# Two-layer hybrid encoder, one core: in layer 2 the weight sums of the seven-product pairs are built in a DRAM scratch by adding DMAs

## The chip, the cores and the metric

The kernel runs on one core of a Trainium2 chip. The metric is the device time of one execution in microseconds (us); the time before is the median of three runs, 1300.78 us (1300.57 to 1301.51). The engines are PE (TensorE, matrix products), DVE (VectorE), ACT (ScalarE), POOL (GpSimd) and SP (SyncE, which here only issues DMAs). Each works through its own queue of instructions in order.

## The reference, cut to what matters

Two encoder layers over 512 positions of width 1024, all in fp32. The change touches only how the third block of layer 2 gets its weights:

```python
for l in range(DEPTH):                      # DEPTH = 2
    x = x + hybrid_mixer(rms_norm(x, ...))              # neighbourhood attention || GQA, then W_out
    x = x + memory_cross_attention(rms_norm(x, ...))    # 4 heads over 256 memory tokens
    x = x + conv_ffn(rms_norm(x, ...), w_up[l], ..., w_down[l])
return rms_norm(x, norm_final)

def conv_ffn(h, w_up, conv_w, conv_b, w_down):          # D_FF = 2816 = 22 chunks of 128
    u = h @ w_up                                        # (512, 1024) @ (1024, 5632)
    u = depthwise_conv_width_3(u)
    gate, val = split(u, 2)
    return (silu(gate) * val) @ w_down
```

## The kernel before

**Arithmetic.** Activations lie transposed, features on the 128 partitions and the 512 positions along the row. PE multiplies in a reduced format (fp32r), so each operand is split into two: `hi` is a rounded copy (ACT), `lo` is the rest, value minus `hi` (DVE or POOL), and a product is three matmuls, hi·hi, hi·lo and lo·hi. Every weight block goes this way: SP loads it from DRAM into a `raw` tile (three buffers, N_RAW), ACT writes `hi`, DVE or POOL subtracts to `lo`, PE uses both. Tiles named `hi` and `lo` have four buffers each (N_W); tiles named `r` and `t` come from wider pools. `plan` lists all weight blocks in the order of use, with a letter for how each is split; `get_w` takes the next block and emits the loads and splits of the blocks ahead.

**The up-projection.** Of the 22 chunks j, the first six of each layer (N_PLAIN) are done as they stand: 48 matmuls of 512 columns for `gate` and `val` together. The other 16 are done as pairs, by a seven-product scheme: `gate` and `val` of a chunk, the two halves of the 1024 input features, and the two halves of the positions make a 2×2 times 2×2 product of blocks, done with seven block products instead of eight, each 4 × 3 matmuls of 256 columns (`product`). The scheme needs seven left operands made of weights: three blocks as they are (`11`, `12`, `22`) and four sums (`s1` to `s4`), and right operands `t1` to `t4` made of activations at the start of the stage (`operands`). In `up(j)` the products run in the order 11, s1, (22 of the pair before), s2, 12, s4, s3. By output tile and left operand they show in the trace as `tr<-r`, `sc<-r,hi`, `tr<-r`, `tr<-r,lo`, `sc<-r`, `sc<-r,hi`, `tr<-r,lo`.

**The weights of a pair.** A pair takes two loads of 512 KB, `first` (letter A) and `second` (letter B). `combined` then splits the three blocks with ACT and DVE (`r<-raw`), lets POOL make the four sums (two adds `t<-raw,raw`, two adds `t<-t,raw`), and splits those with ACT and DVE into halves of `hi` and `lo` tiles (`hi<-t`, `lo<-t`; the DVE half reads what ACT wrote, so it shows as `hi<-t,hi` and `lo<-t,lo`). Beside each pair comes one block of the down-projection (`down_grouped`, 24 matmuls of 512 columns, letter D).

**What sets the order.** All calls are recorded on a `Tape`. `Tape.plan` then runs a list scheduler over the whole program with assumed costs per instruction (`Step`) and with due times counted back from PE's work, in several variants, and `Tape.play` issues the instructions of each engine in the order of the best. So one edit may reorder every queue, also far from where it is made. During attention a `Filler` puts pieces of the projections between the attention steps, so that PE has work while ACT, DVE and POOL do the softmax.

Of the kernel before, what the change touches and what calls it, by code (L numbers as in the profile page):

```python
# [30 lines left out]
D_FF = 2816  # L31
NF = D_FF // P
N_GROUPED = 16
N_PLAIN = 6
N_RAWS = 3
N_COLS = 256
BEHIND = 5
# [64 lines left out]
class Step:  # L102
# [5 lines left out]
    def __init__(self, i, engine, name, call, args, kwargs):  # L108
        self.i, self.engine, self.name, self.call = i, engine, name, (call, args, kwargs)
        self.reads, self.writes = [], []  # L110
        for n, a in [*enumerate(args), *kwargs.items()]:
            if hasattr(a, "tensor") or type(a).__name__ == "Tile":
                a = a if hasattr(a, "ap") and not callable(a.ap) else a[:]
                (self.writes if n in (0, "out", "accum_out") else self.reads).append(a)
        self.needs, self.frees, self.after, self.leads = set(), set(), set(), set()
        self.opens, self.tiles, self.moved = [], [], 0
        if name == "dma_start":
            self.busy = self.length = 450.0
            to, source = self.writes[0], self.reads[0] if self.reads else None
            runs = min(run(a) for a in (to, source) if a is not None)  # L120
            inside = source is not None and type(source.tensor).__name__ == type(to.tensor).__name__ == "Tile"
            rate = 205.0 if to.shape[0] < P or inside else 285.0 if runs < 256 else 340.0 if runs < 512 else 375.0
            self.moved = 4 / rate
            for c in to.shape:
                self.moved *= c
        elif name == "make_identity":
            self.busy = self.length = 1200.0
        else:
            self.busy, self.length = self.times()
        ends = self.reads[:: max(1, len(self.reads) - 1)] if name in TWO_INPUTS else self.reads[:1] + self.writes  # L130
        self.shared = engine == E_POOL and columns(self.writes[0]) > 8 or (
            engine == E_DVE and (name in TWO_INPUTS or name in FAST and (name == "tensor_copy" or columns(self.writes[0]) > 4))
            and all(tag_of(a.tensor) not in IN_PSUM for a in ends))
# [48 lines left out]
class Tape:  # L182


    def __init__(self):
        self.steps, self.tag, self.users, self.opened = [], {}, {}, {}
        self.written, self.read, self.in_order = {}, {}, None

    def take(self, engine, name, call, args, kwargs):
        s = Step(len(self.steps), engine, name, call, args, kwargs)  # L190
        for a, w in [(a, False) for a in s.reads] + [(a, True) for a in s.writes]:
            if type(a.tensor).__name__ == "Tile":
                self.touch(s, a, w)
        if self.in_order is not None and s.moved:
            s.after.update(self.in_order[-1:])
            self.in_order.append(s.i)
        s.needs.discard(s.i)
        s.after -= s.needs | {s.i}
        for x in s.needs:
            self.steps[x].frees.add(s.i)  # L200
        for x in s.after:
# [298 lines left out]
def encoder_kernel(ctx: ExitStack, tc: tile.TileContext, t: dict, out: list):  # L500
# [66 lines left out]
    def operand_of(v, tile, sub):  # L567

# [66 lines left out]
    def stored(*shape):  # L635
        nonlocal at
        n = P * int(np.prod(shape))
        at += n
        v = t["w"][at - n : at]
        return v.rearrange("(p k c) -> p k c", p=P, c=shape[1]) if shape[1:] else v.rearrange("(p c) -> p c", p=P)  # L640

    firsts = [stored(n[2], P) if isinstance(n, tuple) else stored(S + 1) if isinstance(n, int) else
              stored(S // 2 + (n.stop == S)) for n in FIRST]
    for key, name, l, rows, c0, ncol, eng in weights():
        plan.append((key, stored(rows.shape[1], ncol) if len(plan) > 2 else None, rows.shape[1], ncol, eng))

    def get_wide(name):
        return [get_w((name, kq), min(AHEAD, 3 - kq)) for kq in range(4)]
# [263 lines left out]
    for l in range(DEPTH):  # L912
# [608 lines left out]
        def up_first():  # L1521


            us = [[None] * 2 for _ in range(N_PLAIN)]
# [18 lines left out]
            for j in range(2, N_PLAIN):  # L1543
# [4 lines left out]
            for j in range(N_PLAIN - 2, N_PLAIN):  # L1548
                stores.append(finish(j))
            for store in stores:  # L1550
                store()

        H = S // 2
        normed = [None] * KC
# [42 lines left out]
        left, pairs = [], []  # L1597

        def take_pair(j):
            get_w(("up", j, 0))  # L1600
            pairs.append(get_w(("up", j, 1)))

        def up(j):

# [193 lines left out]
            scaled(1)  # L1798

        up_first()  # L1800
        for n in range(N_PLAIN, NF):
            up(n)
            for r in behind(n):
                down_grouped(*divmod(r, 4))
# [30 lines left out]
def weights():  # L1835
# [15 lines left out]
    def pair(j):  # L1851
        gate, val = P * j, D_FF + P * j
        k = list(range(KC))
        return [placed(("up", j, 0), "w_up", k, [gate] * 4 + [val] * 4, "A"),
                placed(("up", j, 1), "w_up", k, [val] * 4 + [gate] * 4, "B")]

# [4 lines left out]
    for l in range(DEPTH):  # L1861
        for n, p in NA_ORDER:
            if n == "v":
                blocks += wide("v", "w_in", 1024, "DPDP")
            else:
                eng = "Dx" if l == 0 and (n, p) in NA_ORDER[:3] else "P"
                blocks.append(cols((n, p), "w_in", 0, KC, (0 if n == "q" else 512) + P * p, P, eng))
        for kh in range(2):
            blocks.append(cols(("gkv", kh), "w_in", 4 * kh, 4, 2048, 256))
        blocks += wide("gq", "w_in", 1536)  # L1870
        for mp in range(4):
            blocks.append(cols(("outn", mp), "w_out", 0, 4, 256 * mp, 256))
        for m in range(4):
            blocks.append(cols(("memk", m), "w_mem_kv", 0, KC, P * m, P))
        blocks += wide("memv", "w_mem_kv", 512)
        p = np.arange(P)[:, None]
        rows = 512 + 256 * (p // HD) + HD * np.arange(4) + p % HD
        for mp in range(4):
            blocks.append((("outg", 0, mp), "w_out", l, rows, 256 * mp, 256, "P"))
        for h in range(4):  # L1880
            blocks.append(cols(("memq", h), "w_mem_q", 0, KC, P * h, P))
        for mp in range(4):
            blocks.append(cols(("memo", 0, mp), "w_mem_o", 0, 4, 256 * mp, 256))
        for n in range(NF):
            blocks += up(n) if n < N_PLAIN else pair(n)
# [80 lines left out]
```

## Time and the profile before

The profiled execution took 1302.85 us, its span was 1300.8 us; 2.05 us lie around the span.

| engine | busy us | share of the span | instructions |
|---|---|---|---|
| PE, matmuls | 1290.8 | 99% | 7557 |
| DVE | 1076.1 | 83% | 2001 |
| ACT | 784.4 | 60% | 1526 |
| POOL | 659.5 | 51% | 527 |

The DMA queues moved 137.48 MB, 106 GB/s on the mean. The granted PE clock was full in every slice of the span.

By the order of the matmuls the span divides so: layer 1's attention and memory block to about 323 us, its feed-forward block to about 650 us, layer 2's attention to about 965 us, and its feed-forward block to the end. The feed-forward block of a layer starts with the six plain chunks; the pairs follow from about 362 us in layer 1 and from about 1000 us in layer 2.

How to read it: matmuls are pipelined and their ends are modelled, so a busy PE says only that it was never seen waiting. Whether a stage runs at PE's rate shows better in the distance of the same step in two neighbouring rounds, or in the two layers, which do the same work. Idle time of the other engines costs nothing by itself.

### The profile page before, as it was taken

The numbers are of one execution on the slowest core, as the hardware profiler recorded it, in microseconds if no ns is written. First come the engines' busy times: TensorE is split into PE (matmuls) and PEld (weight loads), VectorE is DVE, ScalarE is ACT, GpSimd is POOL, SyncE is SP. The second block draws the span as 40 slices with busy tenths as digits, with TensorE's granted clock in tenths as the row PEclk, the third lists the DMA queues.
The fourth block names the chain that finished last, engine by engine and source line by source line (L and its number), as shares of the span: only waits on it lengthen the run. The fifth ranks groups of instructions, "written<-read, shape, count | busy, mean of one in ns | idle before, by whom it ended". The sixth has DMA issues, their size and how long they took to land.

```text
span 1300.8 us, 20807 instructions
## 1 busy us (share of the span) xinstructions
PE 1290.8 (99%) x7557; PEld 1138.5 (88%) x7557; DVE 1076.1 (83%) x2001; ACT 784.4 (60%) x1526; POOL 659.5 (51%) x527
## 2 busy tenths in 40 slices
PE   9999999999999999999999999999999999999998
PEld 7898888888899999999888988888888999999997
DVE  7689885769999999888555897956799999997884
ACT  7776786555665555554537866865646555554552
POOL 4565857716823534433726566765365333452360
PEclk9999999999999999999999999999999999999999
DMA  8741313313224333223355322232132233323231
GB/s 286 224 141 49 105 56 98 98 35 113 81 82 123 105 113 115 66 98 123 112 162 179 115 80 82 65 99 96 49 98 81 82 115 115 128 99 98 97 99 66
DMA packets 42902, 137.48 MB, mean 106 GB/s; under 512 B 5040, under 2 KB 8496, under 8 KB 42800
## 3 DMA queue, kind: packets, MB, share of 16 engines
q1 hardware_dynamic: 42224, 135.51, 32.9%
q8 instruction: 59, 0.97, 0.3%
q10 hardware_dynamic: 576, 0.66, 0.1%
q14 instruction: 43, 0.35, 0.1%
HBM read 126.18 MB, written 2.10 MB: 99 GB/s over the span
## 4 chain that ended last, share of the span: by engine, by line
PE 91%; DVE 5%; issue 2%; POOL 2%; ACT 1%; DVEq 0%; POOLq 0%; ACTq 0%
PE mm L405 52%; PE tr L405 20%; PE sc L405 19%; DVE t L405 2%; DVE r L405 1%; POOL lo L405 1%; DVE lo L405 0%; DVE s L405 0%; POOL s L405 0%; POOL t L405 0%; ACT r L405 0%; ACT t L405 0%; DVE mm L405 0%; DVE xg L405 0%; DVE hi L405 0%
## 5 line engine op out<-in xcount | busy, mean ns | idle before, releaser
L405 POOL TENSOR_TENSOR lo<-raw,hi 128x512 fp32r<-128x512 f32 (+2 forms) x164 | 255.9, 1579 | 161.6 <-ACT hi L405 153.9
L405 PE MATMUL mm<-xg,hi 128*128 128x512 f32 (+1 forms) x930 | 289.7, 392 | 0.0
L405 POOL TENSOR_TENSOR t<-raw,raw 128x512 f32<-128x512 f32 x64 | 99.1, 1569 | 284.2 <-DMA raw<-in_w 231.1
L405 ACT CAST hi<-raw 128x512 fp32r<-128x512 f32 (+2 forms) x212 | 159.6, 779 | 109.2 <-issue 37.2
L405 PE MATMUL mm<-r,hi 128*128 128x512 f32 (+1 forms) x704 | 222.0, 388 | 0.0
L405 PEld LDWEIGHTS mm<-xg,hi 128*128 128x128 f32 x930 | 170.8, 189 | 31.9
L405 PE MATMUL mm<-xg,lo 128*128 128x512 f32 (+1 forms) x465 | 181.3, 390 | 0.0
L405 PEld LDWEIGHTS mm<-r,hi 128*128 128x128 f32 x704 | 130.2, 188 | 25.9 <-DVE xg L405 0.8
L405 PE MATMUL mm<-r,lo 128*128 128x512 f32 (+1 forms) x384 | 141.5, 369 | 0.0
L405 PE MATMUL sc<-r,r 128*128 128x256 f32 (+1 forms) x760 | 133.9, 309 | 0.0
L405 PE MATMUL sc<-r,hi 128*128 128x256 f32 (+1 forms) x832 | 122.9, 291 | 0.8 <-DVE hi L405 0.8
L405 PEld LDWEIGHTS sc<-r,hi 128*128 128x128 f32 x832 | 109.0, 192 | 3.6 <-DVE hi L405 1.0
L405 PEld LDWEIGHTS sc<-r,r 128*128 128x128 f32 x760 | 106.0, 191 | 6.3 <-ACT t L405 0.6
L405 PE MATMUL tr<-r,lo 128*128 128x256 f32 (+1 forms) x784 | 108.9, 285 | 0.0
L405 PE MATMUL mm<-hi,xg 128*128 128x512 f32 (+1 forms) x384 | 108.1, 357 | 0.0
L405 POOL TENSOR_TENSOR t<-t,raw 128x512 f32<-128x512 f32 x64 | 102.7, 1605 | 5.0
L405 PEld LDWEIGHTS mm<-xg,lo 128*128 128x128 f32 x465 | 87.5, 188 | 18.2
L405 POOL TENSOR_SCALAR t<-t,s 128x512 f32<-128x512 f32 (+1 forms) x112 | 66.9, 611 | 71.7 <-DVE s L405 68.4
L405 PE MATMUL tr<-r,r 128*128 128x256 f32 x768 | 102.7, 283 | 0.0
L405 PEld LDWEIGHTS tr<-r,r 128*128 128x128 f32 x768 | 98.9, 191 | 2.6
L405 PEld LDWEIGHTS tr<-r,lo 128*128 128x128 f32 x784 | 99.7, 192 | 0.8
L405 DVE TENSOR_TENSOR r<-raw,r 128x512 fp32r<-128x512 f32 x96 | 91.3, 956 | 0.2 <-ACT r L405 0.2
(160 smaller groups left out, 2697.3 us busy)
## 6 DMA issues: line engine op xcount, KB each, us to landing
raw<-in_w SPq DMA_DIRECT2D x207, 512.0 KB, 3.5
r<-r SPq DMA_DIRECT2D x30, 256.0 KB, 3.6
r<-in_bias SPq DMA_DIRECT2D x16, 384.0 KB, 4.6
raw<-in_w SPq DMA_DIRECT2D x8, 384.0 KB, 3.1
r<-in_memT SPq DMA_DIRECT2D x4, 512.0 KB, 6.7
xT<-in_w SPq DMA_DIRECT2D x7, 256.5 KB, 4.5
r<-in_w SPq DMA_DIRECT2D x9, 128.0 KB, 4.1
t<-in_memT SPq DMA_DIRECT2D x4, 256.0 KB, 6.1
```

Of the source, the lines that this page charges most:

```text
L405: call(*args, **kwargs)
```

## The change

For layer 2 the four sums of each of the 16 pairs are no longer made on the core. During layer 1 every pair gets a scratch tile `made` in DRAM, filled in four steps: SP copies the blocks 22, 11 and 12 into it (DRAM to DRAM, 0.75 MB and 0.25 MB), and three DMAs issued by POOL, which add their source to what lies at the target, make it s1, s2, s3 and s4 (0.75 MB, 0.25 MB, 0.25 MB; the second and third read what the one before wrote). The steps of pair number j are recorded at 90 + 48 j us, and 12 us after one another, of the recorder's count of PE's work; the scheduler may issue them later. In layer 2 a pair is then four blocks, [11, s1], [12, s2], [s3, s4] and [22], each loaded (two of them by two DMAs of 256 KB) and split by one ACT copy and one DVE subtraction into `hi` and `lo` tiles, like a down block. Layer 1 keeps its sums on POOL. `PLAIN = (6, 6)` keeps six plain chunks in both layers, and the two lines that empty `built` find nothing left in it.

```diff
-N_PLAIN = 6
+PLAIN = (6, 6)
+SUMMED = (False, True)
+CHAIN, PITCH, PAUSE = 90000.0, 48000.0, 12000.0
...
             rate = 205.0 if to.shape[0] < P or inside else 285.0 if runs < 256 else 340.0 if runs < 512 else 375.0
+            if engine == E_POOL:
+                self.busy, rate = 1250.0, 165.0
...
+        if engine == E_PE:
+            while self.chores and self.chores[0][0] <= self.pe.ns:
+                n = len(self.steps)
+                self.chores.pop(0)[1]()
+                for x in self.steps[n:]:
+                    x.after.add(s.i)
+                    s.leads.add(x.i)
...
+    dpool = ctx.enter_context(tc.tile_pool(name="dpool", bufs=1, space=DRAM))
...
     def emit_raw():
-        SP.dma_start(*raw_tile())
+        raw, src = raw_tile()
+        k = 0
+        for part in src if isinstance(src, list) else [src]:
+            SP.dma_start(raw[:, k : k + part.shape[1]], part)
+            k += part.shape[1]
...
+    def chain(src):
+        b21, b22, b11, b12 = (src[:, 4 * n : 4 * n + 4] for n in range(4))
+        made = dpool.tile([P, 16, P], F32, name=nm("made"), tag=f"made{len(chains)}")
+        s1, s2, s3, s4 = (made[:, 4 * n : 4 * n + 4] for n in range(4))
+        flat = lambda v: v.rearrange("p k c -> p (k c)")
+
+        def copies():
+            SP.dma_start(made[:, 4:16], src[:, 4:16])
+            SP.dma_start(s1, b22)
+
+        def first():
+            POOL.dma_start(made[:, 0:12].rearrange("p (n k) c -> p n (k c)", n=3),
+                           flat(b21).unsqueeze(1).to_broadcast([P, 3, 4 * P]), accum_op=ALU.add)
+
+        chains.append((copies, first, lambda: POOL.dma_start(s2, b11, accum_op=ALU.add),
+                       lambda: POOL.dma_start(s4, s2, accum_op=ALU.add)))
+        return [b11, s1], [b12, s2], made[:, 8:16], b22
+
     for key, name, l, rows, c0, ncol, eng in weights():
...
+        if eng != "S":
+            plan.append((key, src, nk, ncol, eng))
+            continue
+        for n, part in enumerate(chain(src)):
+            plan.append(((*key, n), part, 8 if n < 3 else 4, ncol, "D"))
+    tape.chores = sorted(((CHAIN + PITCH * j + PAUSE * i, step) for j, c in enumerate(chains) for i, step in enumerate(c)), key=lambda c: c[0])
...
         def take_pair(j):
-            get_w(("up", j, 0))
-            pairs.append(get_w(("up", j, 1)))
+            if not SUMMED[l]:
+                get_w(("up", j, 0))
+                pairs.append(get_w(("up", j, 1)))
+                return
+            w = {}
+            for i, names in enumerate((("11", "s1"), ("12", "s2"), ("s3", "s4"), ("22",))):
+                hi, lo = get_w(("up", j, i))
+                for n, name in enumerate(names):
+                    w[name] = [(hi[:, 4 * n + k], lo[:, 4 * n + k]) for k in range(4)]
+            pairs.append(w)
```

Counted over the program, the matmuls stay 7537. DVE loses 48 subtractions, ACT 48 copies. POOL loses 64 adds and gains 48 DMAs. SP gains 96 DMAs.

Three places in the new order. A row is an instruction, output tile before the arrow, inputs behind it, the number that of the buffer.

POOL in layer 1, before: the sums of two neighbouring pairs, four adds each, stand one behind the other.

```order
L405 TENSOR_TENSOR t_1168<-raw_1131,raw_1150 128x512
L405 TENSOR_TENSOR t_1167<-raw_1131,raw_1150 128x512
L405 TENSOR_TENSOR t_1169<-t_1167,raw_1131 128x512
L405 TENSOR_TENSOR t_1170<-t_1169,raw_1150 128x512
L405 TENSOR_TENSOR t_1193<-raw_1156,raw_1175 128x512
L405 TENSOR_TENSOR t_1192<-raw_1156,raw_1175 128x512
```

POOL at the same two pairs of layer 1, with the change.

```order
L417 TENSOR_TENSOR t_1186<-raw_1149,raw_1168 128x512
L417 TENSOR_TENSOR t_1185<-raw_1149,raw_1168 128x512
L417 TENSOR_TENSOR t_1187<-t_1185,raw_1149 128x512
L417 TENSOR_TENSOR t_1188<-t_1187,raw_1168 128x512
L417 DMA made_87<-in_w 128x3x512
L417 DMA made_87<-in_w 128x512
L417 TENSOR_TENSOR t_1211<-raw_1174,raw_1193 128x512
L417 TENSOR_TENSOR t_1210<-raw_1174,raw_1193 128x512
```

Two adding DMAs now stand between the sums of one pair and those of the next, and the second must wait until the first has landed; at the other pairs one to four adds stand between them.

DVE in layer 2, before: the instructions in front of the subtraction for s1 of the second pair, `hi_2039`.

```order
L405 TENSOR_TENSOR r_2032<-raw_1996,r_2032 128x512
L405 SCALAR_TENSOR_TENSOR t_2019<-mm_1997,par,t_2019 128x504
L405 SCALAR_TENSOR_TENSOR t_2020<-mm_2010,par,t_2020 128x504
L405 TENSOR_TENSOR tr_2029<-tr_2029,t_2031 128x256
L405 TENSOR_TENSOR r_2033<-raw_2009,r_2033 128x512
L405 SCALAR_TENSOR_TENSOR t_2019<-mm_1997,par,t_2019 128x7
L405 SCALAR_TENSOR_TENSOR t_2020<-mm_2010,par,t_2020 128x7
L405 TENSOR_TENSOR t_2017<-t_2017,t_2018 128x512
L405 TENSOR_TENSOR hi_2039<-t_2036,hi_2039 128x512
```

DVE there with the change: `raw_2037` holds 11 and s1 of the second pair.

```order
L417 SCALAR_TENSOR_TENSOR t_2031<-mm_2021,par,t_2031 128x504
L417 SCALAR_TENSOR_TENSOR t_2030<-mm_2017,par,t_2030 128x7
L417 TENSOR_TENSOR t_2028<-t_2028,t_2029 128x512
L417 TENSOR_TENSOR lo_2042<-raw_2020,hi_2041 128x1024
L417 SCALAR_TENSOR_TENSOR t_2030<-mm_2017,par,t_2030 128x504
L417 SCALAR_TENSOR_TENSOR t_2031<-mm_2021,par,t_2031 128x7
L417 TENSOR_TENSOR xg_2033<-t_2028,xg_2032 128x512
L417 TENSOR_TENSOR lo_2045<-raw_2037,hi_2044 128x1024
L417 SCALAR_TENSOR_TENSOR t_2030<-mm_2017,par,t_2030 128x7
L417 SCALAR_TENSOR_TENSOR t_2031<-mm_2021,par,t_2031 128x504
L417 TENSOR_TENSOR tr_2048<-tr_2048,t_2050 128x256
```

The split of s1 now stands ahead of the add into `tr` of the first pair (`tr_2048`; before, `tr_2029` stood ahead of it), and one subtraction of 1024 columns serves 11 and s1.

SP in layer 2, before: the loads of a down block (`raw_1988`), of the second pair (`raw_1996`, `raw_2009`), of the next down block, and the first of the third pair.

```order
L405 DMA raw_1988<-in_w 128x1024
L405 DMA raw_1996<-in_w 128x1024
L405 DMA raw_2009<-in_w 128x1024
L405 DMA raw_2026<-in_w 128x1024
L405 DMA raw_2027<-in_w 128x1024
```

SP in layer 2 with the change: the down block, the second pair, the next down block.

```order
L417 DMA raw_2020<-in_w 128x1024
L417 DMA raw_2037<-in_w 128x512
L417 DMA raw_2037<-made_79 128x512
L417 DMA raw_2040<-in_w 128x512
L417 DMA raw_2040<-made_79 128x512
L417 DMA raw_2043<-made_79 128x1024
L417 DMA raw_2046<-in_w 128x512
L417 DMA raw_2053<-in_w 128x1024
```

A pair and its down block now take five `raw` tiles and seven DMAs; before they took three of each.

More of the change, by code (lines that the diff above doesn't have):

```diff
@@ L187, in __init__ @@
         self.written, self.read, self.in_order = {}, {}, None
+        self.chores, self.pe = [], None
     def take(self, engine, name, call, args, kwargs):
@@ L643, in encoder_kernel @@
               stored(S // 2 + (n.stop == S)) for n in FIRST]
-    for key, name, l, rows, c0, ncol, eng in weights():
-        plan.append((key, stored(rows.shape[1], ncol) if len(plan) > 2 else None, rows.shape[1], ncol, eng))
+    chains = []
+    def chain(src):
[12 more added lines that the diff above has]
+        return [b11, s1], [b12, s2], made[:, 8:16], b22
+    for key, name, l, rows, c0, ncol, eng in weights():
+        nk = rows.shape[1]
+        src = stored(nk, ncol) if len(plan) > 2 else None
+        if eng != "S":
[4 more added lines that the diff above has]
+    tape.chores = sorted(((CHAIN + PITCH * j + PAUSE * i, step) for j, c in enumerate(chains) for i, step in enumerate(c)), key=lambda c: c[0])
+    tape.pe = PE
     def get_wide(name):
@@ L1521, in up_first @@
         def up_first():
-            us = [[None] * 2 for _ in range(N_PLAIN)]
+            us = [[None] * 2 for _ in range(PLAIN[l])]
             up_project(0, 0, range(KC - 1), us[0])
@@ L1542, in up_first @@
             stores = []
-            for j in range(2, N_PLAIN):
+            for j in range(2, PLAIN[l]):
                 for side in range(2):
@@ L1547, in up_first @@
                 stores.append(finish(j - 2))
-            for j in range(N_PLAIN - 2, N_PLAIN):
+            for j in range(PLAIN[l] - 2, PLAIN[l]):
                 stores.append(finish(j))
@@ L1551, in up_first @@
                 store()
+            for _ in built:
+                pass
         H = S // 2
@@ L1800, in encoder_kernel @@
         up_first()
-        for n in range(N_PLAIN, NF):
+        for n in range(PLAIN[l], NF):
             up(n)
@@ L1853, in pair @@
         k = list(range(KC))
+        if SUMMED[l]:
+            return [placed(("up", j), "w_up", 2 * k, [val] * 8 + [gate] * 8, "S")]
         return [placed(("up", j, 0), "w_up", k, [gate] * 4 + [val] * 4, "A"),
@@ L1884, in weights @@
         for n in range(NF):
-            blocks += up(n) if n < N_PLAIN else pair(n)
+            blocks += up(n) if n < PLAIN[l] else pair(n)
             blocks += [grouped(*divmod(r, 4)) for r in behind(n)]
```

## Prediction

> **What bounds the kernel now.** I read the page first: engines and chain, then who PE waits for, then the chain in order of time for both feed-forward stages, then the timeline at the one place of layer 2 where PE waits.
>
> ```profile
> PE 1290.8 (99%) x7557; PEld 1138.5 (88%) x7557; DVE 1076.1 (83%) x2001; ACT 784.4 (60%) x1526; POOL 659.5 (51%) x527
> PE 91%; DVE 5%; issue 2%; POOL 2%; ACT 1%; DVEq 0%; POOLq 0%; ACTq 0%
> ...
> PE tr L405 <- DVE s L405: 1.2, 1, 1.2
> PE sc L405 <- DVE hi L405: 0.8, 1, 0.8
> PE tr L405 <- PEq L1958: 0.8, 1, 0.8
> PE tr L405 <- POOL t L405: 0.5, 1, 0.5
> PE tr L405 <- DVE r L405: 0.4, 1, 0.4
> PE sc L405 <- DVE xg L405: 0.2, 1, 0.2
> ```
>
> PE is busy for 99% of the span, and all its waits with a name come to 1.2 + 0.8 + 0.8 + 0.5 + 0.4 + 0.2 = 3.9 us (total, times, longest). The change leaves the matmuls as they are, so it can only gain from waits. The one that lies in its stage is `sc` for `DVE hi`, 0.8 us. What the wait costs is better read from the chain in order of time (start, length, what), at the same step of the two layers:
>
> ```profile
> 323.43 5.44 PE sc L405 x24
> 399.46 2.88 PE tr L405 x24
> 451.52 2.88 PE tr L405 x24
> 467.06 2.88 PE tr L405 x24
> ...
> 965.23 5.44 PE sc L405 x24
> 1042.54 2.88 PE tr L405 x24
> 1094.67 2.88 PE tr L405 x24
> 1110.21 2.88 PE tr L405 x24
> ```
>
> In layer 1, where no wait of PE falls into this stage, a round of one pair and one down block takes 467.06 − 451.52 = 15.54 us; in layer 2 it takes 1110.21 − 1094.67 = 15.54 us too. So from there on layer 2 already runs at PE's pace, though its sums are made on POOL. Only the way into the stage differs: 399.46 − 323.43 = 76.03 us in layer 1, 1042.54 − 965.23 = 77.31 us in layer 2, for the same matmuls. The entry of layer 2 loses 1.28 us. The timeline shows where:
>
> ```profile
> 1024.11 0.40 PE L405 MATMUL sc<-r,hi 128*128 128x256 f32 x2
> 1025.35 1.46 PE L405 MATMUL sc<-r,hi 128*128 128x256 f32 x10 [0.85 <-DVE hi L405]
> ...
> 1021.48 1.51 DVE L405 TENSOR_TENSOR r<-raw,r 128x512 fp32r<-128x512 f32 x1
> 1023.18 1.51 DVE L405 TENSOR_TENSOR t<-t,t 128x512 f32<-128x512 f32 x1
> 1024.62 0.68 DVE L405 TENSOR_TENSOR hi<-t,hi 128x512 fp32r<-128x512 f32 x1
> 1021.16 2.99 POOL L405 TENSOR_TENSOR t<-t,raw 128x512 f32<-128x512 f32 x2
> ```
>
> PE stops after two of twelve matmuls of product s1 of the second pair, until DVE has subtracted its low part. DVE has no gap there; two of its instructions just ahead took 1.51 us while POOL made sums, and the next of the same size took 0.68 us.
>
> **The change part by part, layer 2.** It takes from each pair four POOL adds and three of seven splits.
>
> ```profile
> L405 POOL TENSOR_TENSOR t<-raw,raw 128x512 f32<-128x512 f32 x64 | 99.1, 1569 | 284.2 <-DMA raw<-in_w 231.1 <-DVE t L405 45.2 <-DVE sc L405 8.0
> L405 POOL TENSOR_TENSOR t<-t,raw 128x512 f32<-128x512 f32 x64 | 102.7, 1605 | 5.0
> L405 DVE TENSOR_TENSOR r<-raw,r 128x512 fp32r<-128x512 f32 x96 | 91.3, 956 | 0.2 <-ACT r L405 0.2
> L405 DVE TENSOR_TENSOR hi<-t,hi 128x512 fp32r<-128x512 f32 x64 | 64.3, 1005 | 10.7 <-ACT hi L405 10.7
> L405 DVE TENSOR_TENSOR lo<-t,lo 128x512 fp32r<-128x512 f32 x64 | 47.4, 752 | 0.3
> ...
> 1000.00:1050.00 50.00, 49.15 (x329) 45.34 (x328) 50.00 (x86) 29.56 (x52) 15.59 (x11) 1.00 0.29 94
> 1050.00:1260.00 210.00, 210.00 (x1453) 196.65 (x1452) 192.31 (x297) 115.59 (x201) 91.38 (x56) 1.00 0.33 107
> ```
>
> POOL loses 2 × 1.569 + 2 × 1.605 = 6.35 us per pair. DVE spends 3 × 0.956 + 2 × 1.005 + 2 × 0.752 = 6.38 us on a pair now. Afterwards it is three subtractions of 1024 columns and one of 512: 3 × 1.22 (the median of such a row of the down blocks, quoted below) + 0.68 = 4.34 us, 2.0 us less. In the stretch 1000 to 1050 DVE is busy 50.00 of 50 us and PE 49.15; these 2.0 us for each of the first two pairs, and the POOL adds that stretch DVE's instructions, go from just the queue PE waits on. In the new order the subtraction with s1 of the second pair stands ahead of the add into the first pair's `tr`, not behind it. Two pairs free 4 us of DVE ahead of a wait of 0.85, so I take the 1.28 us as gone. From 1050 on PE is busy 210.00 of 210 us: the 6.35 us of POOL and 2.0 us of DVE of the other fourteen pairs are worth nothing, since PE's matmuls cover them. ACT's saving (three copies fewer) is covered the same way.
>
> What layer 2 pays is loads. A round brings 7 × 256 KB + 512 KB = 2.36 MB in 15.54 us, 152 GB/s, where it was 1.57 MB and 101.
>
> ```profile
> 0.00:67.00 67.00, 65.01 (x316) 55.34 (x317) 48.14 (x108) 47.85 (x106) 32.82 (x39) 1.00 0.80 252
> L405 SPq DMA_DIRECT2D raw<-in_w x42: 327/328/382, 1054.9 to 1256.8; - x42
> L405 ACT CAST hi<-raw x15: 1042/1052/1058, 1056.5 to 1250.4; 128x1024 fp32r<-128x1024 f32 x15
> L405 DVE TENSOR_TENSOR lo<-raw,hi x13: 1210/1216/1952, 1058.4 to 1229.9; 128x1024 fp32r<-128x1024 f32 x13
> DMA to landing us min/median/max: 3.3/3.6/5.2
> ```
>
> The first 67 us moved 252 GB/s (last column), so bandwidth holds. Buffers: five `raw` tiles a round go through three buffers, so each may be held for 3 × 15.54 / 5 = 9.32 us. Bare, it takes 3.6 (landing) + 1.05 (ACT) + 1.22 (DVE) = 5.9 us, which leaves 3.4 us for standing in queues. Four new issues per round on SP are 4 × 0.33 us, with nothing behind them but later loads. Cost: none, covered by that margin; between none and the rival below.
>
> **Layer 1 and both attentions.** POOL gains 48 DMAs, none of which the trace shows. Ends for what one takes of POOL: 0.33 us (SP's issue above) and 1.6 us (its add); I take 1.6, the row of the same engine, 77 us in all. The cover is POOL's idle time; in layer 1's pair stage POOL waits 6 us for the next load, and what it makes is needed much later:
>
> ```profile
> 448.75 3.01 POOL L405 TENSOR_TENSOR t<-raw,raw 128x512 f32<-128x512 f32 x2 [6.11 <-DMA raw<-in_w]
> 452.88 1.13 DVE L405 TENSOR_TENSOR hi<-t,hi 128x512 fp32r<-128x512 f32 x1
> 465.46 1.60 PE L405 MATMUL sc<-r,hi 128*128 128x256 f32 x12
> ```
>
> The low part of s1 is ready at 454.01, and PE uses it at 465.46: 11.45 us of slack behind 6.11 us of idle time. A POOL DMA that waits for the one before it holds the sums behind it, and these hold ACT, DVE and at last PE, but only beyond 17.5 us. SP's copies go ahead of weight loads and delay them by about two loads (1 MB read and written, 3.6 us for each 512 KB): up to 7 us, inside the same 17.5.
>
> Outside that stage stand 32 of the 48 DMAs (by the new order), most of them in the attentions, where POOL's work is nearer to PE. Two rows give the ends. PE waited for POOL once, 0.5 us (above), beside 659.5 us of POOL's work; in that proportion 77 us cost 0.06. The chain runs through POOL for 2% of the span, 26 us or 3.9% of POOL's work; in that proportion they cost 3.0. I take 0.3, near the first, since it is PE's own waits and the chain counts POOL also where PE had no gap. The scheduler also orders both attentions anew. What another order of the same work is worth, the two layers show:
>
> ```profile
> 67.33 5.09 PE mm L405 x26
> 708.02 5.09 PE mm L405 x26
> ```
>
> From there to the first plain chunk it is 323.43 − 67.33 = 256.10 us in layer 1 and 965.23 − 708.02 = 257.21 in layer 2. So a new order moves a layer by about 1.1 us either way, both layers by 1.6 (root of the sum of squares), with no sign: 0.
>
> **The sum.** The profiled execution took 1302.85 us (span 1300.8 and 2.05 around it): 1302.85 − 1.28 + 0.3 = 1301.87. The median of the runs lies 2.07 below it, so I predict 1300.78 − 1.0 = 1299.8 us. A difference under 0.2%, 2.6 us, can't be told from none.
>
> **The rivals.**
>
> 1. *Late loads in layer 2 (slower).* In the pair stage a `raw` tile waits in SP's, ACT's and DVE's queues longer than 3.4 us. For it: three queues in order, and two half loads must both land. Against it: DVE loses 2.0 us a round. Each 0.1 us above 9.32 stretches a round by 0.17 us and 16 rounds by 2.7; at a cycle of 9.6 us the kernel takes 1299.8 + 7.5 = 1307.
>
> 2. *The adding DMAs hold POOL in layer 1 (slower).* The largest adds 0.75 MB. As plain loads of 512 KB go it takes 1.5 × 3.6 = 5.4 us; if its three streams (source, target read, target written) went one after another, 16.2 us. Two issues and that are 3.2 + 16.2 = 19.4 us, 1.9 beyond the 17.5, at the five pairs of the stage that such a DMA stands in front of: 9.5 us, 1309. At 5.4 it costs nothing. I take 5.4, since a load here too reads and writes its 512 KB within the same 3.6 us. [...]
>
> 3. *DVE keeps POOL from issuing (slower, too little to tell).* The trace has the two holding each other: beside POOL's adds DVE's 0.68 us become 1.51. If each of the 32 DMAs outside the pair stage lost the longest of DVE's rows here, 1.5 us, POOL would lose 48 us, and 3.9% of that reaches the chain: 1299.8 + 1.9 = 1301.7. Against it: a DMA in DRAM gives POOL nothing to read on the core. [...]
>
> 4. *Nothing is gained.* The entry wait comes back as another one: the 1024-column subtraction serves 11 and s1 together, so 11 must wait for more. 1300.78 + 0.3 = 1301.1.
>
> 5. *The new order of attention falls well (faster).* Both layers gain 1.1 us: 1299.8 − 2.2 = 1297.6.
>
> **How the numbers follow.** Forecast (1299.8, own range 1298.2 to 1302.5: a new order, and 3.0 in place of 0.3) 0.58, rival 1 0.09, rival 2 0.09, rival 3 0.07, rival 4 0.07, rival 5 0.10. Faster than 1298.18 (0.2%) are most of rival 5 and the lower edge of the forecast: 0.14. Slower than 1303.38 are rivals 1 and 2 and a bad order: 0.20. The rest, 0.66, is no measurable change. The range leaves out the far parts of rivals 1 and 2 and the lower edge of rival 5: 1297.5 to 1306.5.
>
> **What would show it.** Right: in layer 2 the way from the first `sc` of the plain chunks to the third pair's `tr` is 76.0 us, no PE wait for `DVE hi`, rounds of 15.54 us, DVE below 50.00 of 50 there, POOL nearly idle. Wrong: rounds over 15.54 in layer 2 with PE waiting for `hi` or `lo` (rival 1); rounds over 15.54 in layer 1 with POOL adds late (rival 2); POOL DMAs that take far over 1.6 us; new PE waits between 67 and 323 or 708 and 965 us, where `POOL t` or `POOL lo` ends them.

## The result, and the profile after

The changed kernel took 1311.35 us (median of 4 runs, 1309.87 to 1311.85), the kernel before 1301.14 beside it (1300.57 to 1302.26): ratio 1.0076, 95% interval 1.0058 to 1.0093, about 10 us slower, where 1299.8 was forecast and 1306.5 was the end of the range. The profiled execution took 1311.85 us, its span was 1310.1 (before: 1302.85 and 1300.8).

The page's engine row and the shares of the chain, after:

```profile
PE 1293.5 (99%) x7557; PEld 1139.4 (87%) x7557; DVE 1040.3 (79%) x1953; ACT 777.4 (59%) x1478; POOL 601.6 (46%) x511
...
PE 89%; DVE 9%; ACT 1%; issue 1%; DMA 0%; SPq 0%; POOL 0%; DVEq 0%; ACTq 0%
```

DVE has 35.8 us less to do and POOL 57.9, as meant, but the chain goes through DVE for 9% of the span, before 5%. Who PE waited for (total, times, longest):

```profile
PE tr L417 <- ACT t L417: 2.1, 1, 2.1
PE tr L417 <- POOL t L417: 1.9, 1, 1.9
PE sc L417 <- ACT t L417: 1.5, 2, 1.0
PE tr L417 <- DVE t L417: 1.3, 2, 0.8
PE tr L417 <- PEq L2017: 0.8, 1, 0.8
PE mm L417 <- DVE xg L417: 0.6, 1, 0.6
PE tr L417 <- DVE tr L417: 0.6, 1, 0.6
...
```

The wait for `DVE hi` is gone, and 3.9 us of waits have become about 10. The chain in order of time, at the steps shown of before:

```profile
974.81 5.44 PE sc L417 x24
...
1050.89 2.88 PE tr L417 x24
...
1066.43 2.88 PE tr L417 x24
```

The way into layer 2's pair stage is 1050.89 − 974.81 = 76.08 us (before 77.31, forecast 76.0), a round 1066.43 − 1050.89 = 15.54, unchanged. The stretch of the pair stage (length, then busy times of PE, PEld, DVE, ACT and POOL, granted clock, DMA share, GB/s):

```profile
1050.00:1260.00 210.00, 210.00 (x1452) 196.59 (x1451) 162.01 (x252) 109.33 (x160) 0.00 (x0) 1.00 0.48 152
```

PE is busy throughout, DVE 162 us where it was 192, POOL not at all, at the 152 GB/s that were forecast. So the stage that was changed behaves as predicted, but for its last round (see `order_alone` below). The loss is ahead of it: layer 2's plain chunks start at 974.81 us, before at 965.23.

What the new DMAs took, by their issues (KB each, median us to landing), and POOL's own time for them (ns, minimum, median, maximum):

```profile
raw<-in_w SPq DMA_DIRECT2D x175, 512.0 KB, 3.7
made<-in_w SPq DMA_DIRECT2D x16, 768.0 KB, 6.5
made<-in_w POOLq DMA_DIRECT2D x16, 768.0 KB, 11.2
```

```profile
L417 POOL DMA_DIRECT2D made<-in_w x32: 831/1060/1444, 113.4 to 908.8; - x32
L417 POOL DMA_DIRECT2D made<-made x16: 785/819/976, 154.0 to 916.2; - x16
its engine sat idle before it (us, times) until:
  DMA made<-in_w: 44.4, 8
...
```

POOL's issue costs about 1 us, less than the 1.6 taken; the 768 KB add lands after 11.2 us, where 5.4 was taken.

### The profile page after: what moved, and what is told of

It is laid out like the page before. It is cut to its first block, busy times and chain, and to the rows that moved or that the text cites. A ratio compares the mean times of both kernels' runs of the same rounds, so it can differ in the third digit from the quotient of the medians.

```text
span 1310.1 us, 20898 instructions
## 1 busy us (share of the span) xinstructions
PE 1293.5 (99%) x7557; PEld 1139.4 (87%) x7557; DVE 1040.3 (79%) x1953; ACT 777.4 (59%) x1478; POOL 601.6 (46%) x511
## 4 chain that ended last, share of the span: by engine, by line
PE 89%; DVE 9%; ACT 1%; issue 1%; DMA 0%; SPq 0%; POOL 0%; DVEq 0%; ACTq 0%
PE mm L417 53%; PE tr L417 18%; PE sc L417 18%; DVE t L417 4%; DVE r L417 2%; DVE s L417 1%; DVE xg L417 0%; ACT t L417 0%; DVE mm L417 0%; DMA xT<-in_w 0%; DVE sc L417 0%; SPq L417 0%; DVE lo L417 0%; DVE hi L417 0%; ACT hi L417 0%
## 5 line engine op out<-in xcount | busy, mean ns | idle before, releaser
L417 ACT CAST hi<-raw 128x1024 fp32r<-128x1024 f32 (+2 forms) x276 | 220.2, 818 | 160.7 <-PE mm L417 92.4
L417 DVE TENSOR_TENSOR lo<-raw,hi 128x1024 fp32r<-128x1024 f32 (+1 forms) x112 | 125.0, 1119 | 40.5 <-ACT hi L417 40.1
L417 PE MATMUL sc<-r,hi 128*128 128x256 f32 (+1 forms) x832 | 142.2, 291 | 0.0
L417 PE MATMUL tr<-r,lo 128*128 128x256 f32 (+1 forms) x656 | 130.8, 287 | 2.4 <-ACT t L417 2.1
L417 PE MATMUL sc<-r,r 128*128 128x256 f32 (+1 forms) x568 | 107.4, 316 | 1.5 <-ACT t L417 1.5
L417 PE MATMUL tr<-r,hi 128*128 128x256 f32 (+1 forms) x544 | 104.2, 289 | 0.6 <-DVE tr L417 0.6
L417 POOL TENSOR_TENSOR t<-raw,raw 128x512 f32<-128x512 f32 x32 | 48.2, 1525 | 102.3 <-DMA raw<-in_w 55.8
L417 PEld LDWEIGHTS sc<-r,r 128*128 128x128 f32 x568 | 82.2, 190 | 8.8 <-ACT t L417 2.7
L417 PEld LDWEIGHTS tr<-r,hi 128*128 128x128 f32 x544 | 86.9, 191 | 3.3 <-DVE tr L417 0.8
L417 ACT ACTIVATE t<-sc,s,s 128x512 f32<-128x512 f32 (+1 forms) x96 | 67.9, 710 | 31.2 <-DVE s L417 30.8
## 6 DMA issues: line engine op xcount, KB each, us to landing
made<-in_w POOLq DMA_DIRECT2D x16, 768.0 KB, 11.2
```

The lines of the kernel that those rows point to most:

```text
L417: call(*args, **kwargs)
```

## Experiments: the order or the DMAs

Theory A: the planner's new order costs the 10 us by itself. Theory B: the DMAs do. In four kernels the two are taken apart; the order of PE, DVE and ACT is instruction for instruction that of the changed kernel in the first two and that of the kernel before in the third.

`order_alone`: the calls are dropped after the plan is made.

```diff
             call, args, kwargs = self.steps[i].call
+            if writes the scratch: continue
+            if loads from the scratch: args = args[0], the same columns of in_w
             call(*args, **kwargs)
```

> The changed kernel with its program order kept instruction for instruction, but with none of the 80 DMAs that write the DRAM scratch; layer 2 loads other columns of the weights in the place of the sums (same sizes, wrong values). Theory A (the planner's new order costs the 10 us: it holds PE up by itself): 1308 to 1312 us, with PE waits at 124 to 141, at 376 and at 806 us as in the changed kernel. Theory B (the DMAs cost it: POOL is held by issuing and waiting, and transfers slow what runs beside them): 1299 to 1302 us and these waits gone.

`no_adds`: only the adding DMAs are dropped.

```diff
+            if kwargs.get("accum_op") is not None:
+                continue
```

> The changed kernel, same order, with SyncE's 32 copies into the scratch but without POOL's 48 adding DMAs (the sums lack their second and third terms). Theory A: 1308 to 1312, as with the adds. Theory B with POOL as the place: as fast as with no scratch at all, 1299 to 1302. Theory B with memory traffic as the place: the copies move 1 MB of the 2.25 MB that a pair's building writes, so about half of what the DMAs cost stays, 1304 to 1307.

`adds_in_old_order`: the kernel before, its plan untouched; the scratch DMAs are issued from `play` after the PE step at which `Tape.take` would have recorded them.

```diff
             call(*args, **kwargs)
+            while self.added and self.added[0][0] == step.i:
+                self.added.pop(0)[1]()
```

> The kernel before with every instruction in its old order, and the same 32 copies and 48 adding DMAs put in at the same counts of PE time; layer 2 doesn't use what they make and sums on POOL as before. Theory A: the DMAs alone cost next to nothing, 1301 to 1303. Theory B: they cost what they cost in the changed kernel, about 1309 to 1313, with new PE waits in both attentions that POOL's or ACT's results end.

`layer2_alone`: no scratch in the plan at all.

```diff
-        return [b11, s1], [b12, s2], made[:, 8:16], b22
+        return [b11, b21], [b12, b22], src[:, 0:8], b22
```

> The half of the change in layer 2 alone: four blocks a pair are loaded and split, in the place of the sums stand other columns of the weights (wrong values), no scratch is written, and the planner orders the program without any of its DMAs. If layer 2's part is worth what I forecast, the way from the first plain sc to the third pair's tr is 76.0 us and the time 1.3 below the kernel before, 1299.5 to 1300, plus or minus what a new order of the attentions brings (layer 1's is new here too, in fewer places). Theory A has this order, too, free to be several us off; theory B has it at 1298.5 to 1301.

| run | us | ratio to before | 95% |
|---|---|---|---|
| order_alone | 1304.33 | 1.0023 | 1.0014 to 1.0033 |
| no_adds | 1304.48 | 1.0024 | 1.0015 to 1.0033 |
| adds_in_old_order | 1337.81 | 1.0287 | 1.0265 to 1.0308 |
| layer2_alone | 1302.70 | 1.0011 | 1.0002 to 1.0020 |

Neither theory holds alone. The copies by SP cost nothing (1304.48 against 1304.33). The adds cost 1.0076 − 1.0023 = 0.53%, 6.9 us, in the order that was planned around them, and 36.5 us (with the copies) in an order that was not. Where the planner, which had assumed 1.25 us of POOL and 165 GB/s for each, had placed them, they cost some 30 us less. And the changed kernel's order without any of them is still 3.0 us slower than before. The chain of `order_alone` at the same two steps, and ahead of them at two of layer 1's and layer 2's that the prediction shows of before (399.46 and 708.02 us there):

```profile
402.51 2.88 PE tr L423 x24
...
710.15 5.09 PE mm L423 x26
...
967.42 5.44 PE sc L423 x24
...
1043.54 2.88 PE tr L423 x24
```

The way in is 76.12 us, so 1.2 us are won there; but the plain chunks start 2.2 us later than before. This is lost in layer 1: its third pair's `tr` comes 402.51 − 399.46 = 3.05 us late, and its attention now has four waits of PE between 125 and 279 us, of 0.4 to 1.0 us, for `ACT t` and `DVE t` (before one, of 0.4). Some 0.9 us come back before 710 us, and layer 2's attention takes as long as before (257.27 against 257.21 us). What follows the third pair's `tr` in layer 2 takes 1302.7 − 1043.54 = 259.16 us of the span against 1300.8 − 1042.54 = 258.26; there PE waits 0.6 us for `DVE tr` in the last round, where before it did not wait. The adds move that start from 967.42 to 974.81, 7.39 us, and the rest hardly (1310.1 − 1050.89 = 259.21). `layer2_alone`, a third order, has its way in in 76.03 us too and is still 0.11% slower than before, not 1.3 us faster as was expected.

## Experiments: which adds, and by what

Where the order on PE is the same, each matmul of one run can be set beside the same matmul of another. Between `order_alone` and the changed kernel nearly the whole lag arises at three places: 3.8 us between 376 and 384 us, 2.1 at 808, 0.9 at 849. The timeline of the changed kernel there (start, length, what; idle time in brackets):

```profile
338.00 1.32 POOL L417 DMA_DIRECT2D made<-in_w  x1
...
338.81 4.62 DVE L417 SCALAR_TENSOR_TENSOR t<-t,t 128x256 f32<-128x256 f32 x1
338.87 2.89 POOL L417 TENSOR_TENSOR lo<-raw,hi 128x1024 fp32r<-128x1024 f32 x1
...
341.23 1.23 POOL L417 TENSOR_TENSOR t<-t 128x256 f32<-128x256 f32 x1
...
341.92 1.22 POOL L417 TENSOR_TENSOR t<-t,t 128x256 f32<-128x256 f32 x1
...
378.74 0.62 PE L417 MATMUL tr<-r,lo 128*128 128x256 f32 x3 [2.06 <-ACT t L417]
...
806.68 0.88 POOL L417 DMA_DIRECT2D made<-in_w  x1 [4.21 <-DMA made<-in_w]
...
808.34 0.66 PE L417 MATMUL tr<-ident,t 128*128 128x128 f32 x4 [1.88 <-POOL t L417]
...
845.14 3.85 POOL L417 TENSOR_TENSOR lo<-raw,hi 128x512 fp32r<-128x512 f32 x3
...
845.91 3.38 DVE L417 TENSOR_TENSOR r<-t,r 128x256 fp32r<-128x256 f32 x1
```

and of `order_alone` at the first of them:

```profile
337.89 2.40 POOL L423 TENSOR_TENSOR lo<-raw,hi 128x1024 fp32r<-128x1024 f32 x1
338.69 1.89 DVE L423 SCALAR_TENSOR_TENSOR t<-t,t 128x256 f32<-128x256 f32 x1
340.25 0.93 POOL L423 TENSOR_TENSOR t<-t 128x256 f32<-128x256 f32 x1
```

The DVE instruction here, which reads two tiles of the core, ends in both runs 0.29 us behind an instruction of POOL: behind POOL's `lo` without the DMA (1.89 us), behind the last of three POOL instructions with it (4.62). DVE has few gaps from there to 378 us, and the 2.7 us stay: set side by side, every DVE instruction up to there comes some 2.9 us late. Then PE stops for 2.06 us. The other 1.7 of the 3.8 us come right behind the stop, where PE waits for nothing. From 380 to 384 us, `order_alone` first (length, busy times of PE, PEld, DVE, ACT and POOL with matmuls and instructions in brackets, granted clock, DMA share, GB/s):

```profile
380.00:384.00 4.00, 4.00 (x22) 3.44 (x21) 4.00 (x8) 0.21 (x1) 3.84 (x3) 1.00 0.03 10
```

```profile
380.00:384.00 4.00, 4.00 (x14) 3.29 (x14) 4.00 (x8) 2.23 (x4) 3.25 (x2) 0.59 0.42 133
```

The granted clock is 0.59 there, which over 4 us is worth 4 × (1 − 0.59) = 1.6 us. So this stop costs nearly twice its length. Not every one does: behind the stop of 1.88 us at 808 us the clock stays at 1.00, and a later run (`no_landing_ring`) parts the two. (In tenths, as on the page, such a drop doesn't show: 9 stands for 90% and more.)

At 845.91 the same happens, 3.38 us in place of 0.79, and PE is 0.9 us late. At 806.68 it is a landing: the second add of a pair waits 4.21 us for the first, and the softmax's scaling, which PE waits for, stands behind it. Theory B1: an add costs only where it falls in front of something urgent.

`four_out`:

```diff
+            if accum_op and its number in (12, 15, 40, 42): continue
```

> The changed kernel, same order, with 4 of POOL's 48 adding DMAs left out (those at 338.0, 384.1, 806.7 and 842.6 us of its trace; the sums of three pairs lack a term). Theory B1 (the adds cost only where one of them falls in front of something urgent: at 338.81 a DVE instruction of 0.41 us lasts 4.62 behind POOL's queue, at 806.68 POOL waits 4.2 us for the add before to land): nearly all of the 7 us goes, 1304 to 1306. Theory B2 (a cost spread over all adds): 4/48 of 7 us, 1310.5 to 1311.

`no_landing`: the add of pair j goes into the scratch of pair j−1, j−2 or j−3.

```diff
+                    to, b12 = self.scratch[j - 1 - part][0], self.scratch[j][1]
```

> The changed kernel, same order and as many bytes, but each of POOL's adding DMAs from the fourth pair on adds into the scratch of another pair, whose last write was begun tens of us before (wrong sums), so that none waits for the one ahead of it. If POOL's waits for landings (44.4 us in the changed kernel, 8 times) cost the 7 us: 1304 to 1305. If only the one at 806.7 does: 1309, the PE wait of 1.9 us for POOL gone, the stop at 376 us still there. If none does: 1311.

`narrow_adds`, and `narrow_in_old_order` alike:

```diff
+                args = [a[:, :, 0:4] if a.shape[1] == 3 else ...[:, 0:4] for a in args]
```

> The changed kernel, same order and same 48 adding DMAs with as many rows, but each row 16 bytes wide in place of 2 KB (the sums are wrong in the rest). If the bytes cost the 7 us (traffic, slow landing): 1304 to 1305 and landings near 3 us. If POOL's issuing does (0.8 to 1.3 us each and what it does to DVE): 1309 to 1311, the 806 us wait gone with the short landing, the stop at 376 us kept. Beside it, POOL's 128x512 instructions that take 1.0 in place of 0.69 us while an add is in flight: they stay slow if writing the rows' descriptors slows POOL, and are 0.69 again if the traffic does.

> The kernel before in its old order with the 32 copies and 48 adding DMAs put in, the adds 16 bytes a row wide. With full rows it took 36.5 us more than before. If the bytes are the cost: 1301 to 1305. If issuing is: 1325 to 1337. In between: the difference is what landings and traffic cost.

| run | us | ratio to before | 95% |
|---|---|---|---|
| four_out | 1304.54 | 1.0022 | 1.0013 to 1.0032 |
| no_landing | 1311.78 | 1.0078 | 1.0061 to 1.0095 |
| narrow_adds | 1309.07 | 1.0058 | 1.0043 to 1.0073 |
| narrow_in_old_order | 1324.98 | 1.0177 | 1.0162 to 1.0192 |

Without 4 of the 48 adds the whole 6.9 us are gone: 1304.54 is `order_alone`'s 1304.33. With all 48 there but almost no bytes, 2.3 us go: the stop at 806 us, while the DVE instructions still take 4.62 and 3.38. So in the changed kernel about 4.7 us come from issuing on POOL and what that does to DVE (with the 1.6 us of lower clock that follow), about 2 from the slow landing. In the old order 23.4 of the 36.5 us are still there without the bytes, the lower edge of what was expected if issuing is the cost. Of the 36.5 us with full rows about 9 are the clock: its mean over the span of 1334.0 us is 0.991, before it is 0.998. Why DVE did not end between POOL's three instructions is not shown.

`no_landing` gained nothing, and its trace says why: POOL stood idle all the same, with nothing in the profile that it waited for.

```profile
its engine sat idle before it (us, times) until:
  issue: 39.0, 7
...
```

`no_landing_ring` asks whether that is room in the scratch that the program reserves for POOL's DMAs:

```diff
-    nc = bacc.Bacc("TRN2", ..., dynamic_dma_scratch_size=1024)
+    nc = bacc.Bacc("TRN2", ..., dynamic_dma_scratch_size=2048)
```

> The run with independent targets again (1311.78 us), with the scratch that the program reserves for the descriptors of POOL's DMAs doubled from 1024 to 2048 bytes. There POOL still stood idle 39.0 us in 7 places ahead of an adding DMA with no semaphore to wait for, one of them the 3.5 us at 806.4 us. If it waited for room for its descriptors: these waits shrink below 10 us and the time falls by the 1.4 us that the 806 us wait costs, to 1310.4. If not: 39 us and 1311.8 again.

The 39.0 us are gone (no such row is left) and with them the stop at 806 us; but the run took 1315.87 us (ratio 1.0104, 1.0091 to 1.0118), for PE now stops for `DVE hi` in layer 1's pair stage, 3.5 us in two waits (at 390 and 508 us). That these waits end with the larger scratch is shown; the forecast of the time was wrong: without them, something else came late.

This run also parts a stop from the clock behind it. The stop near 380 us is there, 2.05 us long, but the clock stays at 1.00, and the matmuls fall 2.3 us behind those of `order_alone`, not 3.8. Behind its new stop of 2.1 us at 508 us the clock falls to half for 3.4 us, and there they lose 3.9 (the clock's mean over the span is 0.997, in `order_alone` 0.999).

## Experiments: the old order kept

To part the new order from the rest, the program order of the kernel before was kept, as a list in the kernel, up to 961 us of its plan, and from there the order planned for four blocks a pair was taken.

`kept_order_bare`:

```diff
     def plan(self, log=None):
+        return the list: before's order up to 961 us, then layer2_alone's
```

> Layer 2's half alone, with the program order of the kernel before kept as it was up to the planned start of layer 2's plain chunks (961 us of the plan), and from there the order planned for four blocks a pair; no scratch, other weights in the place of the sums (wrong values). If the way into layer 2's pair stage is worth its 1.28 us and the rest of the losses lie in the new order of the attentions: the first sc of the plain chunks to the third pair's tr in 76.0 us, and a time 1.3 us below the kernel before (ratio 0.999). If the new order before 961 us had nothing to do with it: 1302.5 to 1304, as in the two runs without any scratch DMA.

It took 1299.85 us against 1301.81, ratio 0.9986 (0.9977 to 0.9994): faster. Its chain:

```profile
964.50 5.44 PE sc L421 x24
...
1040.53 2.88 PE tr L421 x24
```

Again 76.03 us for the way in, and this time nothing is lost ahead of it. The run is 0.14% faster, about 1.8 us, and measured against it the changed kernel's own order costs 1.0023 − 0.9986 = 0.37%, 4.8 us (layer2_alone's: 0.25%, 3.3 us).

Not all of the 1.8 us is layer 2's. The profiled spans differ by 2.0 us, of which 1.28 are the way in. Another 0.9 arise at 652 us, at the end of layer 1's feed-forward block, where both runs have the same instructions. DVE there, before and in `kept_order_bare`:

```profile
650.48 2.25 DVE L405 TENSOR_TENSOR t<-t,t 128x512 f32<-128x512 f32 x1 [0.77 <-ACT t L405]
```

```profile
650.66 1.00 DVE L421 TENSOR_TENSOR t<-t,t 128x512 f32<-128x512 f32 x1 [0.77 <-ACT t L421]
```

Before, DVE ends only 0.54 us behind the last of three POOL subtractions, here between them. It takes 1.00 us in the profile of every run with the kept order; why is not shown. So by the profiles layer 2's half by itself is worth about 1.3 us, 0.10%, which the interval of the runs holds as well.

Could the whole change live in that order? By B1, yes, if the adds stand where POOL is idle. `kept_order` put them into the two pair stages:

```diff
+        at = 1.0, 1.6, range(9)          # layer 1: first round, rounds per pair, pairs
+        if l:
+            at = 1.0, 1.5, range(9, 16)
+        tape.chores = sorted((PE.ns + 15500.0 * (at[0] + at[1] * (j - at[2][0])) + ..., step) ...)
```

> The same order with the whole change's work: all 32 copies and 48 adding DMAs are there, but put where POOL's results are not urgent, nine pairs' during layer 1's pair stage (a pair every 24.8 us) and seven during layer 2's (one every 23.3 us), by the count of PE time. Theory B1 (a DMA on POOL costs only in front of urgent work): the same as without them, 1299.5 to 1301, the reference's result and a ratio near 0.999. If the adds cost wherever they stand (bytes, DVE held), or layer 2's loads come late beside them: 1303 to 1310, with PE waits inside the pair stages.

It took 1346.71 us, ratio 1.0345 (1.0329 to 1.0362), the worst of all and far beyond both forecasts. The matmuls fall behind by 18 us between 400 and 600 us and by 25 between 1100 and 1225, some 12 of these 43 us through the clock (0.990 on the mean, without the adds 0.999). In the second stretch loads of `raw` took 3.1/6.4/11.3 us to land (minimum, median, maximum from 1050 to 1260 us; without the adds 2.6/3.5/5.2). The third run put them into POOL's gaps:

```diff
+            if step.engine == E_POOL:
+                pool += 1
+                while adds and adds[0][0] == pool:   # ADDS: (POOL instruction, pair, part)
+                    self.parts[adds[0][1]][adds.pop(0)[2] + 1]()
```

> The kept order with the whole change's work, as in the run before, but each adding DMA stands where POOL's queue had a gap of at least 2.4 us in the run without them, one in flight at a time (16 us after a pair's first, 9 after the others): 43 of 48 from 94 to 946 us, mostly one pair per 40 to 60 us, five in layer 2's pair stage. If an adding DMA costs by what stands behind it on POOL and by crowding beside loads, both are avoided: 1299.5 to 1302, ratio 0.999 to 1.0. If adds beside layer 1's pair stage cost in themselves (17 of them are there): 1303 to 1310.

1320.06 us, ratio 1.0140 (1.0123 to 1.0157), beyond both forecasts: B1 doesn't say all. The largest stop, on the timeline:

```profile
431.61 1.28 POOL L691 DMA_DIRECT2D made<-in_w  x1
431.69 5.62 SPq L424 DMA_DIRECT2D raw<-in_w  x3
...
446.84 0.62 ACT L424 CAST r<-raw 128x512 fp32r<-128x512 f32 x1 [8.61 <-DMA raw<-in_w]
...
449.49 0.80 PE L424 MATMUL tr<-r,lo 128*128 128x256 f32 x2 [5.92 <-ACT t L424]
```

The second of the three loads went out at 435.18 us, beside the 768 KB add, and landed 11.6 us later. ACT waited 8.61 us for it, and the ACT instruction that PE needed stood behind it. The landings of `raw` from 323 to 660 us, first without the adds, then with them:

```profile
DMA to landing us min/median/max: 2.8/3.5/4.9
```

```profile
DMA to landing us min/median/max: 2.8/3.9/11.6
```

Theory B3: besides what stands behind it on POOL, an add costs by its bytes beside urgent loads. Two more runs put that to the test; `kept_gaps_narrow` has the same places and 16 bytes a row, `kept_places` full rows and another list of places.

```diff
-ADDS = [(POOL instruction, pair, part), ...]     # a third of them in layer 1's pair stage
+ADDS = [...]                                     # 6 there, 39 in the attentions and layer 1's last down blocks, 3 in layer 2
```

> The run before (adds in POOL's gaps, 1320.06 us) with the adds 16 bytes a row wide (the sums are wrong in the rest). Theory B1 (an add costs by what stands behind it on POOL, and POOL's gaps avoid that), with the bytes as what was left: loads beside an add landed in up to 11.6 us there, 4.9 without adds; then 1300 to 1302, loads at 3.5 and below 6.5 us again. If issuing still costs in the gaps: 1310 to 1320.

> The whole change's work in the kept order once more, the adds in POOL's gaps again, but only two pairs' in layer 1's pair stage (at places where the run before lost nothing), one pair's in layer 2's, the other thirteen pairs' in the attentions and layer 1's last down blocks, where loads are few. If the bytes beside the pair stage's loads were what the run before lost: 1300 to 1302.5, a ratio of 0.9985 to 1.0005. If adds cost anywhere: 1310 and more.

The narrow adds took 1300.54 us, ratio 0.9988 (0.9979 to 0.9997): all 48 issues in POOL's gaps cost under 1 us, and the other 19.5 were the bytes and what followed from them. Mostly out of the loads' way, with full rows, it took 1306.57 us, 1.0036 (1.0024 to 1.0047), between its two forecasts: 13.5 of the 19.5 us are back, not all. What is left lies at 225 (1.7 us, PE waits for POOL's `r`), 382 (1.2), 516 (0.9) and 723 us (0.8); it was not followed further. No version that really makes the sums beat the kernel before; two that leave the sums or nearly all their bytes out did, by 0.14 and 0.12%.

## Why the prediction was wrong

- *The entry, −1.28 us: right.* 77.31 became 76.08 us, and 76.0 to 76.1 in the runs above with four blocks a pair that show both steps (not in `kept_gaps`, where two adds stand just ahead and PE stops for 2.0 us at 1027 us). The run that has little else, `kept_order_bare`, is 0.14% faster (0.06 to 0.23), but 0.9 us of that lie in layer 1.
- *The rest of layer 2 hidden, its loads covered: right up to the last round.* Rounds of 15.54 us, POOL at 0.00, PE busy 210.00 of 210 us. The end of the stage, which the sum left out, costs 0.9 us in this order; in `kept_order_bare` it costs nothing. Rival 1 needs loads that are slow, and `kept_order` shows them (6.4 us to land at the median, 3.5 without the adds).
- *New order of the attentions, 0 with 1.6 either way: wrong.* It cost 4.8 us against the kept order (`layer2_alone`'s 3.3). By the profiles 3.05 us of it are lost in layer 1 up to the third pair's `tr`, nothing in layer 2's attention. The step that failed took the difference of two layers within one plan, 1.1 us, for the scatter between plans, and gave it no sign. Both new orders timed here were slower; that the plan before was one that fell well is a guess from three orders.
- *48 POOL DMAs, +0.3 with ends of 0.06 and 3.0: wrong.* They cost 6.9. The size of an issue was right (1.06 and 0.82 us at the median for 1.6 taken), its price was not: I priced POOL's added time in proportion to what POOL's work had cost PE so far. What the runs showed in its place: 44 cost next to nothing and 4 cost everything, through three things that no share shows: DVE, held behind POOL with a full queue of its own (4.7 us in all), a POOL DMA that waits for the one before it (about 2), and, within the 4.7, a lower clock behind the longest stop (1.6).
- *Landing of the 768 KB add, 5.4 us: wrong,* 11.2. In the pair stage of layer 1 the 17.5 us of slack still covered it, as the text said, and rival 2 didn't come true (a round there takes 15.54 us); in layer 2's attention, at 806 us, there was no such slack, and the text had looked for it in one stage only.
- *SP's copies within the slack: right,* 0.15 us of difference.
- *Rival 3: the wrong way round.* The 48 issues took 1444 ns at most (medians 1060 and 819), where the rival added 1.5 us to each of 32; it was DVE that was held (4.62 us in place of 1.89).
- *The signs:* of those named for a wrong forecast, a new PE wait for `POOL t` between 708 and 965 us came true.

## What to carry to other kernels

Work that is moved to an idle engine is not priced by that engine's free share: look at the instructions that stand behind each of its new places, at the engine that it holds up (here DVE), and at the loads in flight beside it. And a stop of PE can cost more than its length: here one of 2.06 us cost 3.8, one of 1.88 us 2.1. Where a planner orders the whole program anew, the new order is a change of its own; keep the old order once, by hand, to learn what the change itself is worth. And a gap in a queue is not a free place for a transfer: here 48 issues in the gaps cost under 1 us, and their bytes 19.5.

## What the runs showed of the hardware

- In the changed kernel a DMA from POOL that adds 768 KB in DRAM landed after 11.2 us at the median (6 KB in as many rows, in `narrow_adds`: 3.6), a copy of as many bytes by SP after 6.5. Weight loads landed in up to 11.6 us beside the adds of `kept_gaps`, in up to 4.9 in `kept_order_bare` without adds (323 to 660 us).
- In `no_landing` POOL stood idle ahead of an adding DMA for 39.0 us in 7 places although the profile shows nothing that it waited for; with `dynamic_dma_scratch_size` doubled from 1024 to 2048, in `no_landing_ring`, this was gone.
- POOL's own 128x512 scalings took longer beside the adds: 752 ns on the mean over 64 in the changed kernel, where the same order without them (`order_alone`) has 696. With the copies by SP alone (`no_adds`) it stays 698, with the narrow adds it is 733, so the bytes account for the smaller part.
- Behind some stops of PE the granted clock fell for a few us: behind the one of 2.06 us near 378 us of the changed kernel it is 0.59 from 380 to 384 us, and 3.8 us are lost. In `no_landing_ring` it stays at 1.00 behind the same stop, and 2.3 us are lost. What decides it is not shown.
